# Row sums of a ReLU: two-pass steps of near-equal length, a partly fused sixth transfer, and another split of the last row between two engines

## The chip, the cores and the metric

The kernel runs on one core of a Trainium2 chip. The metric is the device time of one execution in microseconds (us). An execution also has a traced span, which is shorter than its time; the difference is called "time less span" below.

## The reference

```python
x = np.random.randn(32, 512, 1024).astype(np.float32)
def reference(x):
    return np.sum(np.maximum(x, 0), axis=-1).astype(np.float32)
```

67.1 MB are read and 64 KB are written. Each of 128 partitions holds 128 rows of 1024 numbers.

## The kernel before

The 128 rows of a partition arrive in seven transfers of 16 rows (three buffers in turn), then in pieces of 8, 4, 2 and 1 rows, then the last row as two halves. SyncE issues all transfers on one queue.

There are two ways to do a row. In two passes, ScalarE writes the ReLU back for several rows in one instruction and VectorE adds them up with one reduce. Fused, one instruction of either engine does ReLU and sum of one row, and leaves the sum in an accumulator that a short second instruction reads out.

```python
STEPS = [2, 6, 8]
TAIL = [8, 4, 2, 1]
LAST = [512, 512]
# ... allocation, and the transfers on SyncE: transfer c waits for s_dve of transfer c - 3 ...

    for c in range(NTWO):                      # transfers 1 to 6: two passes
        b, r = c % NB, 0
        act.wait_ge(s_in[c], 16)
        for i, n in enumerate(STEPS):
            t = buf[:, b, r : r + n, :]
            act.activation(t, t, AF.Relu).then_inc(s_act, 1)
            dve.wait_ge(s_act, len(STEPS) * c + i + 1)
            dve.tensor_reduce(out=res[...], in_=t, axis=X, op=ALU.add).then_inc(s_dve, 1)
            r += n
    # ... on_act(t, acc), on_dve(t, acc): the fused row on ScalarE, on VectorE ...
    for c in range(NTWO, NBIG):                # transfer 7: fused, rows in turn
        act.wait_ge(s_in[c], 16)
        dve.wait_ge(s_in[c], 16)
        for i in range(BIG):
            f = on_act if i % 2 else on_dve
            f(buf[:, c % NB, i, :], res[...])
    for r, n, s in tail:                       # pieces of 8, 4, 2, 1 rows: the same,
        act.wait_ge(s, 16)                     # the single row on ScalarE
        if n > 1:
            dve.wait_ge(s, 16)
        for i in range(r, r + n):
            f = on_act if n == 1 or (i - r) % 2 else on_dve
            ...
    last_act.then_inc(s_tact, 1)

    dve.wait_ge(s_in[-2], 16)                  # last row, first half: VectorE
    on_dve(buf[:, tb, BIG - 1, 0 : LAST[0]], last[:, LAST[1] : LAST[1] + 1]).then_inc(s_part, 1)
    dve.wait_ge(s_part, 1)
    dve.wait_ge(s_in[-1], 16)                  # second half and the partial sum beside it
    on_dve(last[:, :], res[:, J - 1 : J]).then_inc(s_tdve, 1)

    sp.wait_ge(s_tact, 1)
    sp.wait_ge(s_tdve, 1)
    sp.dma_start(out=ov[:, :], in_=res[:, :]).then_inc(s_out, 16)
```

Of the kernel before, what the change touches and what calls it, by code (L numbers as in the profile page):

```python
# [2 lines left out]

P = 128
D = 1024
BIG = 16
NBIG = 7
NTWO = 6
NB = 3
STEPS = [2, 6, 8]  # L10
TAIL = [8, 4, 2, 1]
LAST = [512, 512]


def bass_relu_sum_kernel(
    nc: bass.Bass,
    x: bass.AP,
    out: bass.AP,
):




    fp32 = mybir.dt.float32
    ALU = mybir.AluOpType
    AF = mybir.ActivationFunctionType
    X = mybir.AxisListType.X

    B, S, _ = x.shape
    J = B * S // P  # L30
    assert BIG * NBIG + sum(TAIL) + 1 == J and sum(LAST) == D

    xv = x.rearrange("b s d -> (b s) d").rearrange("(p j) d -> p j d", p=P)
    ov = out.rearrange("b s -> (b s)").rearrange("(p j) -> p j", p=P)

    buf = nc.alloc_sbuf_tensor("buf", [P, NB, BIG, D], fp32)
    last = nc.alloc_sbuf_tensor("last", [P, LAST[1] + 1], fp32)
    res = nc.alloc_sbuf_tensor("res", [P, J], fp32)

    n_in = NBIG + len(TAIL) + 2  # L40
    s_in = [nc.alloc_semaphore(f"s_in{i}") for i in range(n_in)]
    s_act = nc.alloc_semaphore("s_act")
    s_dve = nc.alloc_semaphore("s_dve")
    s_part = nc.alloc_semaphore("s_part")
    s_tact = nc.alloc_semaphore("s_tact")
    s_tdve = nc.alloc_semaphore("s_tdve")
    s_out = nc.alloc_semaphore("s_out")

    sp, act, dve = nc.sync, nc.scalar, nc.vector


    tb = NBIG % NB
    for c in range(NBIG + 1):
        if c >= NB:
            sp.wait_ge(s_dve, len(STEPS) * (c - NB + 1))
        if c < NBIG:
            sp.dma_start(  # L57
                out=buf[:, c % NB, :, :], in_=xv[:, c * BIG : (c + 1) * BIG, :]
            ).then_inc(s_in[c], 16)
    r = 0  # L60
    tail = []
    for i, n in enumerate(TAIL):
        sp.dma_start(
            out=buf[:, tb, r : r + n, :],
            in_=xv[:, NBIG * BIG + r : NBIG * BIG + r + n, :],
        ).then_inc(s_in[NBIG + i], 16)
        tail.append((r, n, s_in[NBIG + i]))
        r += n
    sp.dma_start(
        out=buf[:, tb, r, 0 : LAST[0]], in_=xv[:, J - 1, 0 : LAST[0]]  # L70
    ).then_inc(s_in[-2], 16)
    sp.dma_start(out=last[:, 0 : LAST[1]], in_=xv[:, J - 1, LAST[0] : D]).then_inc(
        s_in[-1], 16
    )


    for c in range(NTWO):
        b, r = c % NB, 0
        act.wait_ge(s_in[c], 16)
        for i, n in enumerate(STEPS):  # L80
            t = buf[:, b, r : r + n, :]
            act.activation(t, t, AF.Relu).then_inc(s_act, 1)  # L82
            dve.wait_ge(s_act, len(STEPS) * c + i + 1)
            dve.tensor_reduce(  # L84
                out=res[:, c * BIG + r : c * BIG + r + n], in_=t, axis=X, op=ALU.add
            ).then_inc(s_dve, 1)
            r += n


    def on_act(t, acc):  # L90
        return act.activation(t, t, AF.Relu, accum_out=acc)  # L91

    def on_dve(t, acc):
        return dve.tensor_scalar(  # L94
            out=t, in0=t, scalar1=0.0, scalar2=None, op0=ALU.max, op1=ALU.add, accum_out=acc
        )

    j0 = NBIG * BIG
    for c in range(NTWO, NBIG):
        act.wait_ge(s_in[c], 16)  # L100
        dve.wait_ge(s_in[c], 16)
        for i in range(BIG):
            f = on_act if i % 2 else on_dve
            f(buf[:, c % NB, i, :], res[:, c * BIG + i : c * BIG + i + 1])
    for r, n, s in tail:
        act.wait_ge(s, 16)
        if n > 1:
            dve.wait_ge(s, 16)
        for i in range(r, r + n):
            f = on_act if n == 1 or (i - r) % 2 else on_dve  # L110
            ins = f(buf[:, tb, i, :], res[:, j0 + i : j0 + i + 1])
            if f is on_act:
                last_act = ins
    last_act.then_inc(s_tact, 1)

    dve.wait_ge(s_in[-2], 16)
    on_dve(buf[:, tb, BIG - 1, 0 : LAST[0]], last[:, LAST[1] : LAST[1] + 1]).then_inc(s_part, 1)
    dve.wait_ge(s_part, 1)
    dve.wait_ge(s_in[-1], 16)
    on_dve(last[:, :], res[:, J - 1 : J]).then_inc(s_tdve, 1)  # L120


    sp.wait_ge(s_tact, 1)
    sp.wait_ge(s_tdve, 1)
    sp.dma_start(out=ov[:, :], in_=res[:, :]).then_inc(s_out, 16)
    sp.wait_ge(s_out, 16)


# [1 line left out]
_INS = ['x']  # L130
_OUTS = [((32, 512), 'float32')]


# [21 lines left out]
```

## Time and profile before

| | before |
|---|---|
| time, median of 3 | 164.67 us (164.54 to 165.19) |
| traced span of the profiled execution | 162.82 us |
| input queue's share of 16 DMA engines | 96.1% |
| seventh transfer taken up by ScalarE | 139.32 us |
| VectorE done with the sixth transfer | 142.72 us |
| final VectorE instruction starts | 160.46 us |

The page of the kernel before, its engines and its queue (busy us, share of the span, records; then packets, MB, share):

```profile
DVE 123.1 (76%) x52; ACT 102.7 (63%) x51; POOL 0.2 (0%) x4
...
q1 hardware_dynamic: 2016, 67.18, 96.1%
```

The queue is full and no engine is. Large transfers land 19.36 us apart, which is 433 GB/s (8.39 MB each). The Trainium skill, "DMA: Bandwidth & Descriptors", Specifications, gives a fabric ceiling of 435 GB/s, and this trace stays just below it. As long as the stream stays as it is, only what comes after the last landing can be shortened.

The timeline of the kernel before, cut to what the end needs (start us, duration us, engine, line, operation, operands, count, idle time before and what ended it):

```profile
119.96 14.04 ACT L82 ACTIVATE buf<-buf 128x2048 f32<-128x2048 f32 x3 [5.31 <-DMA buf<-in_x_dram]
...
134.03 8.69 DVE L84 TENSOR_REDUCE res<-buf 128x8 f32<-128x8192 f32 x1 [0.36 <-ACT buf L82]
139.32 1.06 ACT L91 ACTIVATE buf<-buf 128x1024 f32<-128x1024 f32 x1 [5.32 <-DMA buf<-in_x_dram]
...
142.64 1.21 DVE L94 TENSOR_SCALAR_CACHE_REDUCE buf<-buf 128x1024 f32<-128x1024 f32 x1
...
158.59 1.21 DVE L94 TENSOR_SCALAR_CACHE_REDUCE buf<-buf 128x1024 f32<-128x1024 f32 x1
...
159.73 0.68 DVE L94 TENSOR_SCALAR_CACHE_REDUCE buf<-buf 128x512 f32<-128x512 f32 x1
...
160.46 0.69 DVE L94 TENSOR_SCALAR_CACHE_REDUCE last<-last 128x513 f32<-128x513 f32 x1
161.07 0.08 DVE L94 DVE_READ_ACCUMULATOR last<-last 128x1 f32 x1
161.24 0.35 SPq L125 DMA_DIRECT2D out_dram<-res  x1
```

The seventh transfer has landed by 139.32, where ScalarE takes it up, but VectorE reduces the sixth until 142.72. From there on it does a row every 1.14 us and its instructions carry no idle time in brackets: it has a backlog. The last half row lands at about 158.9 (issued at 125.71, 33.2 us to landing), and VectorE comes to it 1.5 us later. Its line among the DMA issues (size, us from issue to landing):

```profile
last<-in_x_dram SPq DMA_DIRECT2D x1, 256.0 KB, 33.2
```

The waits of VectorE in the kernel before (us in total, times, longest) say the same: it never waited for a transfer.

```profile
DVE res L84 <- ACT buf L82: 38.0, 13, 25.1
```

So does the chain of work that ended last (start, us, what). After the sixth transfer's last reduce it is VectorE's own work:

```profile
134.03 8.69 DVE res L84
142.72 16.28 DVE buf L94 x29
...
160.46 0.69 DVE last L94 x2
```

### The profile page before, as it was taken

What the parts mean: (1) busy time and instruction counts of PE and PEld (TensorE: products, weight loads), DVE (VectorE), ACT (ScalarE), POOL (GpSimd) and SP (SyncE); (2) the same over time, 40 slices, a digit from 0 to 9 for tenths busy, and PEclk for the clock granted to TensorE, in tenths of its full rate; (3) what the DMA queues carried; (4) which work ended last, traced back from release to release, by engine and by line L of the source; (5) the groups of instructions that cost most, each with busy time, mean ns of one, the idle gap of its engine ahead of it and who ended that gap; (6) DMA issues with size and microseconds to landing.
All of it is one profiled execution on the core that took longest, in us unless ns stands there. A gap on an engine that the chain in (4) does not pass through costs nothing.

```text
span 162.8 us, 136 instructions
## 1 busy us (share of the span) xinstructions
DVE 123.1 (76%) x52; ACT 102.7 (63%) x51; POOL 0.2 (0%) x4
## 2 busy tenths in 40 slices
DVE  0000005599988999599996999969998799999995
ACT  3000039991599807996099942999159990796880
POOL 0000000000000000000000000000000000000000
DMA  7979979979989998998997997997998997999980
GB/s 258 515 306 467 499 322 467 515 322 451 515 370 403 515 419 354 515 419 354 515 467 306 515 499 322 467 515 338 435 515 354 419 515 338 427 419 403 411 322 16
DMA packets 2016, 67.18 MB, mean 413 GB/s; under 512 B 224, under 2 KB 352, under 8 KB 736
## 3 DMA queue, kind: packets, MB, share of 16 engines
q1 hardware_dynamic: 2016, 67.18, 96.1%
HBM read 67.11 MB, written 0.07 MB: 413 GB/s over the span
## 4 chain that ended last, share of the span: by engine, by line
DMA 47%; ACT 26%; DVE 22%; another core or an unknown queue 3%; issue 1%; SPq 0%
DMA buf<-in_x_dram 47%; ACT buf L82 26%; DVE res L84 11%; DVE buf L94 10%; DVE last L94 0%; SPq L57 0%
## 5 line engine op out<-in xcount | busy, mean ns | idle before, releaser
L84 DVE TENSOR_REDUCE res<-buf 128x2 f32<-128x2048 f32 (+2 forms) x18 | 104.7, 5839 | 38.0 <-ACT buf L82 38.0
L82 ACT ACTIVATE buf<-buf 128x2048 f32<-128x2048 f32 (+2 forms) x18 | 84.2, 4743 | 47.7 <-DMA buf<-in_x_dram 47.7
L91 ACT ACTIVATE buf<-buf 128x1024 f32<-128x1024 f32 x16 | 16.7, 1045 | 7.7 <-DMA buf<-in_x_dram 7.5
L94 DVE TENSOR_SCALAR_CACHE_REDUCE buf<-buf 128x1024 f32<-128x1024 f32 (+1 forms) x16 | 17.8, 1180 | 0.0
L91 ACT ACTIVATION_READ_ACCUMULATOR buf<-buf 128x1 f32 x16 | 3.0, 187 | 0.0
L82 ACT ACT_TABLE_LOAD x1 | 1.3, 1283 | 0.7 <-PEq L140 0.7
L94 DVE DVE_READ_ACCUMULATOR buf<-buf 128x1 f32 x16 | 1.3, 82 | 0.0
L94 DVE TENSOR_SCALAR_CACHE_REDUCE last<-last 128x513 f32<-128x513 f32 x1 | 0.7, 690 | 0.0
L140 POOL MEMSET const-bfloat16-1.0<- 128x1 bf16 x1 | 0.1, 102 | 0.0
L140 POOL MEMSET const-uint8-127<- 128x1 uint8 x1 | 0.1, 101 | 0.0
L140 POOL MEMSET const-float32-0.0<- 128x1 f32 x1 | 0.1, 99 | 0.2 <-issue 0.2
L140 POOL MEMSET const-float32-1.0<- 128x1 f32 x1 | 0.1, 98 | 0.0
L94 DVE DVE_READ_ACCUMULATOR last<-last 128x1 f32 x1 | 0.1, 82 | 0.0
## 6 DMA issues: line engine op xcount, KB each, us to landing
buf<-in_x_dram SPq DMA_DIRECT2D x1, 4096.0 KB, 25.6
buf<-in_x_dram SPq DMA_DIRECT2D x1, 2048.0 KB, 30.1
buf<-in_x_dram SPq DMA_DIRECT2D x1, 1024.0 KB, 32.1
buf<-in_x_dram SPq DMA_DIRECT2D x1, 512.0 KB, 32.9
buf<-in_x_dram SPq DMA_DIRECT2D x1, 256.0 KB, 33.1
last<-in_x_dram SPq DMA_DIRECT2D x1, 256.0 KB, 33.2
buf<-in_x_dram SPq DMA_DIRECT2D x7, 35.3
out_dram<-res SPq DMA_DIRECT2D x1, 64.0 KB, 1.5
```

The lines of the kernel that those rows point to most:

```text
L82: act.activation(t, t, AF.Relu).then_inc(s_act, 1)
L84: dve.tensor_reduce(out=res[:, c * BIG + r : c * BIG + r + n], in_=t, axis=X, op=ALU.add).then_inc(s_dve, 1)
L91: return act.activation(t, t, AF.Relu, accum_out=acc)
L94: return dve.tensor_scalar(out=t, in0=t, scalar1=0.0, scalar2=None, op0=ALU.max, op1=ALU.add, accum_out=acc)
L140: nc = _bacc.Bacc("TRN2", target_bir_lowering=False, num_devices=1)
```

## The change

The steps of the two-pass transfers become 4, 5, 7, so that the last reduce is shorter. In the sixth transfer only 12 rows go in two passes (3, 4, 5), and VectorE and ScalarE do two fused rows each. The single-row piece goes to VectorE. ScalarE does the last row's first half and hands its partial sum to VectorE's final instruction. The output transfer now waits for one semaphore, since the final instruction implies the rest.

```diff
-STEPS = [2, 6, 8]
+STEPS = [4, 5, 7]
+MIXED = [3, 4, 5]
 ...
+    for c in range(NTWO):
+        b, steps = c % NB, STEPS if c < NTWO - 1 else MIXED
+        act.wait_ge(s_in[c], 16)
+        if steps is MIXED:
+            dve.wait_ge(s_in[c], 16)
+            for i in (BIG - 4, BIG - 3):
+                on_dve(*row(c, i))
+        # ... the steps, as before ...
+        if steps is MIXED:
+            for i in (BIG - 2, BIG - 1):
+                on_act(*row(c, i))
 ...
-            f = on_act if n == 1 or (i - r) % 2 else on_dve
+            f = on_act if (i - r) % 2 else on_dve
 ...
-    dve.wait_ge(s_in[-2], 16)
-    on_dve(buf[:, tb, BIG - 1, 0 : LAST[0]], last[:, LAST[1] : LAST[1] + 1]).then_inc(s_part, 1)
-    dve.wait_ge(s_part, 1)
+    act.wait_ge(s_in[-2], 16)
+    on_act(buf[:, tb, BIG - 1, 0 : LAST[0]], last[:, LAST[1] : LAST[1] + 1]).then_inc(s_tact, 1)
+    dve.wait_ge(s_tact, 1)
     dve.wait_ge(s_in[-1], 16)
     on_dve(last[:, :], res[:, J - 1 : J]).then_inc(s_tdve, 1)
 
-    sp.wait_ge(s_tact, 1)
     sp.wait_ge(s_tdve, 1)
```

More of the change, by code (lines that the diff above doesn't have):

```diff
@@ L43, in bass_relu_sum_kernel @@
     s_dve = nc.alloc_semaphore("s_dve")
-    s_part = nc.alloc_semaphore("s_part")
     s_tact = nc.alloc_semaphore("s_tact")
@@ L54, in bass_relu_sum_kernel @@
         if c >= NB:
-            sp.wait_ge(s_dve, len(STEPS) * (c - NB + 1))
+            sp.wait_ge(s_dve, 3 * (c - NB + 1))
         if c < NBIG:
@@ L74, in bass_relu_sum_kernel @@
     )
-    for c in range(NTWO):
-        b, r = c % NB, 0
-        act.wait_ge(s_in[c], 16)
-        for i, n in enumerate(STEPS):
-            t = buf[:, b, r : r + n, :]
-            act.activation(t, t, AF.Relu).then_inc(s_act, 1)
-            dve.wait_ge(s_act, len(STEPS) * c + i + 1)
-            dve.tensor_reduce(
-                out=res[:, c * BIG + r : c * BIG + r + n], in_=t, axis=X, op=ALU.add
-            ).then_inc(s_dve, 1)
-            r += n
     def on_act(t, acc):
@@ L96, in on_dve, with row @@
         )
+    def row(c, i):
+        return buf[:, c % NB, i, :], res[:, c * BIG + i : c * BIG + i + 1]
+    for c in range(NTWO):
[5 more added lines that the diff above has]
+                on_dve(*row(c, i))
+        r = 0
+        for i, n in enumerate(steps):
+            t = buf[:, b, r : r + n, :]
+            act.activation(t, t, AF.Relu).then_inc(s_act, 1)
+            dve.wait_ge(s_act, 3 * c + i + 1)
+            dve.tensor_reduce(
+                out=res[:, c * BIG + r : c * BIG + r + n], in_=t, axis=X, op=ALU.add
+            ).then_inc(s_dve, 1)
+            r += n
+        if steps is MIXED:
+            for i in (BIG - 2, BIG - 1):
+                on_act(*row(c, i))
     j0 = NBIG * BIG
@@ L102, in bass_relu_sum_kernel @@
         for i in range(BIG):
-            f = on_act if i % 2 else on_dve
-            f(buf[:, c % NB, i, :], res[:, c * BIG + i : c * BIG + i + 1])
+            (on_act if i % 2 else on_dve)(*row(c, i))
     for r, n, s in tail:
-        act.wait_ge(s, 16)
         if n > 1:
-            dve.wait_ge(s, 16)
+            act.wait_ge(s, 16)
+        dve.wait_ge(s, 16)
         for i in range(r, r + n):
-            f = on_act if n == 1 or (i - r) % 2 else on_dve
-            ins = f(buf[:, tb, i, :], res[:, j0 + i : j0 + i + 1])
-            if f is on_act:
-                last_act = ins
-    last_act.then_inc(s_tact, 1)
-    dve.wait_ge(s_in[-2], 16)
-    on_dve(buf[:, tb, BIG - 1, 0 : LAST[0]], last[:, LAST[1] : LAST[1] + 1]).then_inc(s_part, 1)
-    dve.wait_ge(s_part, 1)
+            f = on_act if (i - r) % 2 else on_dve
+            f(buf[:, tb, i, :], res[:, j0 + i : j0 + i + 1])
+    act.wait_ge(s_in[-2], 16)
+    on_act(buf[:, tb, BIG - 1, 0 : LAST[0]], last[:, LAST[1] : LAST[1] + 1]).then_inc(s_tact, 1)
+    dve.wait_ge(s_tact, 1)
     dve.wait_ge(s_in[-1], 16)
     on_dve(last[:, :], res[:, J - 1 : J]).then_inc(s_tdve, 1)
-    sp.wait_ge(s_tact, 1)
     sp.wait_ge(s_tdve, 1)
```

## The prediction

> **What bounds it.** The input stream. The page's queue part gives one queue 67.18 MB, 96.1% of 16 engines' span. The timeline shows ScalarE released by each 8.39 MB transfer at 23.15, 42.45, 61.91, 81.28, 100.61, 119.96 and 139.32 us: 19.36 us apart, 433 GB/s. The Trainium skill, "DMA: Bandwidth & Descriptors", Specifications, gives a fabric ceiling of 435 GB/s; the trace agrees, so no compute order can speed up the stream. The queue never runs dry: the fourth transfer is issued at 45.93 us, when the first buffer is free, while the third is in flight until 61.91. What can be won is only what follows the last landing.
>
> **The end.** From issue and time to landing (DMA issues), the last row's first half lands near 158.33 us and its second near 158.92. The final VectorE instruction starts only at 160.46, so about 1.5 us is lost. The reason is backlog: the sixth transfer's last reduce (8 rows, 8.69 us) runs until 142.72, 3.4 us after the seventh landed. From 142.64 VectorE runs rows 1.14 us apart without a gap to 160.4 (groups: idle before 0.0). ScalarE is idle before each tail piece and done at 158.8.
>
> **What the change does.**
> 1. Steps 4,5,7. Reduce durations (by form: 2278, 6553, 8686 ns for 2, 6, 8 rows) fit about 145 + 1.043 ns per element: 4.42, 5.49, 7.62 us. ScalarE's fit the skill's "ScalarE: Activation LUTs" figure of 186 ns + 0.833 per element (8192: 7010 against 7012 ns measured), so its total stays about 14.05 us. VectorE's last reduce starts where it did (landing + 14.06), but is 7.6 instead of 8.7 us: VectorE ends about 21.7 us after a landing, not 22.75. The buffers come free 1 us earlier; nobody waits for them, so this is worth about 0 by itself.
> 2. Sixth transfer: VectorE, free 2.35 us after landing (119.96), does two fused rows (2.3 us), then reduces of 3, 4, 5 rows (3.35 + 4.42 + 5.49): done near 137.9 instead of 142.72, thus before the seventh lands. ScalarE finishes 12 + 2 rows at about 132.5. This removes the backlog.
> 3. Seventh: eight rows on VectorE 139.35 to 148.5, idle till 149.03; then four rows to about 153.65, two from 153.95 to 156.2, one from 156.43 to 157.65; the single-row piece (now VectorE) 157.67 to 158.9. It keeps pace with the landings.
> 4. The first half goes to ScalarE: starts near 158.36; estimate 0.61 us plus accumulator read, ending near 159.08. VectorE's final instruction waits for this (about 0.15 us longer than for its own landing), runs 159.1 to 159.8, against 160.46 to 161.15.
>
> On the critical path: about 1.35 us in total, nearly all from item 2 together with 3 and 4; the remainder of the changes is hidden under the stream. Without 4, the half row (0.6 us) and final would end near 160.2, so 4 is worth about 0.4 of it.
>
> **Prediction.** Span 162.8 to 161.45; the time 164.67 to 163.3 us (0.8% faster). Range 162.9 to 163.9. Faster by over 2%: 0.02; within 2%: 0.97; slower by over 2%: 0.01.
>
> **What would show it.** Landings of all seven large transfers unchanged within 0.1 us or so; VectorE's last reduce done near 138; VectorE idle before the seventh transfer and before each tail piece; final instruction starting near 159.1, released by ScalarE; chain of waits ending DMA, ScalarE half row, VectorE final.
>
> **What would make it wrong.** A stream whose landings shift (by the earlier issues, or by chance) by more than 0.5 us; VectorE not done with the single-row piece by 159.1; the accumulator reaching VectorE later than ScalarE's fit says; or a spread between runs (164.54 to 165.19 before) that hides a gain of this size.

## The result, and the profile after

| | before | after |
|---|---|---|
| time, median | 164.61 us (4 runs) | 162.93 us (4 runs, 162.74 to 163.03) |
| ratio, 95% interval | | 0.9889 (0.9864 to 0.9913) |
| traced span, profiled execution | 162.82 us | 161.37 us |
| time less span, profiled execution | 1.74 us | 1.55 us |

A ratio here is the mean time of one kernel's runs over that of the other's in the same rounds, so it is not quite the ratio of the medians. The prediction's own ratio, 163.3 over 164.67, is 0.9917: just outside this interval. The gain is larger than foretold. The median of 162.93 us lies at the lower edge of the stated range of 162.9 to 163.9; 0.9889 of the 164.67 us from which the prediction started would be 162.84, just below it.

The timeline of the changed kernel, for the same stretch:

```profile
119.92 10.63 ACT L99 ACTIVATE buf<-buf 128x3072 f32<-128x3072 f32 x3 [5.30 <-DMA buf<-in_x_dram]
122.19 1.21 DVE L82 TENSOR_SCALAR_CACHE_REDUCE buf<-buf 128x1024 f32<-128x1024 f32 x1
...
124.47 13.07 DVE L101 TENSOR_REDUCE res<-buf 128x3 f32<-128x3072 f32 x3
...
139.27 1.22 DVE L82 TENSOR_SCALAR_CACHE_REDUCE buf<-buf 128x1024 f32<-128x1024 f32 x1 [1.74 <-DMA buf<-in_x_dram]
...
157.65 1.22 DVE L82 TENSOR_SCALAR_CACHE_REDUCE buf<-buf 128x1024 f32<-128x1024 f32 x1
158.31 0.63 ACT L79 ACTIVATE buf<-buf 128x512 f32<-128x512 f32 x1 [0.80 <-DMA buf<-in_x_dram]
...
158.85 0.19 ACT L79 ACTIVATION_READ_ACCUMULATOR buf<-buf 128x1 f32 x1
159.07 0.69 DVE L82 TENSOR_SCALAR_CACHE_REDUCE last<-last 128x513 f32<-128x513 f32 x1 [0.19 <-ACT buf L79]
159.68 0.08 DVE L82 DVE_READ_ACCUMULATOR last<-last 128x1 f32 x1
159.79 0.35 SPq L132 DMA_DIRECT2D out_dram<-res  x1
```

VectorE is done with the sixth transfer at 137.54 (124.47 + 13.07) and waits 1.74 us for the seventh: the backlog is gone. At the end ScalarE's half row releases the final instruction at 159.07. The prediction had 137.9 and 159.1.

VectorE's waits in the changed kernel now name the transfers:

```profile
DVE res L101 <- ACT buf L99: 34.9, 10, 26.8
DVE buf L82 <- DMA buf<-in_x_dram: 2.5, 3, 1.7
DVE last L82 <- ACT buf L79: 0.2, 1, 0.2
```

The end of the chain that ended last, in the changed kernel (start, us, what), runs as foretold: landing, ScalarE, final instruction.

```profile
124.16 34.13 DMA buf<-in_x_dram
158.29 0.02 issue
158.31 0.73 ACT buf L79 x2
159.04 0.02 issue
159.07 0.69 DVE last L82 x2
```

The page of the changed kernel:

```profile
DVE 122.0 (76%) x56; ACT 101.0 (63%) x55; POOL 0.2 (0%) x4
...
q1 hardware_dynamic: 2016, 67.18, 97.0%
```

So the trace is almost exactly what was predicted, and the time is not. Note x52 and x56 in the two pages: VectorE has four records (instructions in the trace) more: two fused rows, two records each. That seemed to be of no interest.

### The profile page after: what moved, and what is told of

Its sections match the earlier page's. It is cut to its first block, busy times and chain, and to the rows that moved or that the text cites. A ratio compares the mean times of both kernels' runs of the same rounds, so it can differ in the third digit from the quotient of the medians.

```text
span 161.4 us, 143 instructions
## 1 busy us (share of the span) xinstructions
DVE 122.0 (76%) x56; ACT 101.0 (63%) x55; POOL 0.2 (0%) x4
## 4 chain that ended last, share of the span: by engine, by line
DMA 69%; ACT 18%; DVE 10%; SPq 1%; issue 0%
DMA buf<-in_x_dram 69%; ACT buf L99 17%; DVE res L101 9%; SPq L64 1%; ACT buf L79 0%; DVE last L82 0%; SPq L58 0%
## 5 line engine op out<-in xcount | busy, mean ns | idle before, releaser
L101 DVE TENSOR_REDUCE res<-buf 128x4 f32<-128x4096 f32 (+3 forms) x18 | 100.4, 5603 | 34.9 <-ACT buf L99 34.9
L99 ACT ACTIVATE buf<-buf 128x4096 f32<-128x4096 f32 (+3 forms) x18 | 80.8, 4553 | 47.7 <-DMA buf<-in_x_dram 47.7
L79 ACT ACTIVATE buf<-buf 128x1024 f32<-128x1024 f32 (+1 forms) x18 | 18.4, 1021 | 9.7 <-DMA buf<-in_x_dram 9.7
L82 DVE TENSOR_SCALAR_CACHE_REDUCE buf<-buf 128x1024 f32<-128x1024 f32 x18 | 21.0, 1217 | 2.7 <-DMA buf<-in_x_dram 2.5
```

Of the source, the lines that this page charges most:

```text
L79: return act.activation(t, t, AF.Relu, accum_out=acc)
L82: return dve.tensor_scalar(out=t, in0=t, scalar1=0.0, scalar2=None, op0=ALU.max, op1=ALU.add, accum_out=acc)
L101: dve.tensor_reduce(out=res[:, c * BIG + r : c * BIG + r + n], in_=t, axis=X, op=ALU.add).then_inc(s_dve, 1)
```

## The experiments

Eighteen experiments ran. Three of them (again, again_2, again_3) are the changed kernel itself, and one kernel ran twice (three_pieces). The seventh transfer is taken up between 139.08 and 139.55 us from profile to profile, so spans of two profiles differ by some tenths through the stream alone. To take that out, the column "end" is the start of the final VectorE instruction less the start of the first ScalarE instruction on the seventh transfer. "Out" is the time from the end of the final instruction's accumulator read to the output transfer's issue. Both are from the profiled execution. "Time less span" is the mean over the kernel's own timed executions. "Records" are VectorE's.

| kernel | end, us | out, us | records | time less span, us | ratio (95%) |
|---|---|---|---|---|---|
| before | 21.14 | 0.09 | 52 | 1.73 | 1 |
| after | 19.80 | 0.03 | 56 | 1.53 | 0.9889 (0.9864 to 0.9913) |
| again | 19.80 | 0.03 | 56 | 1.61 | 0.9910 (0.9896 to 0.9924) |
| again_2 | 19.79 | 0.03 | 56 | 1.57 | 0.9905 (0.9890 to 0.9920) |
| again_3 | 19.78 | 0.04 | 56 | 1.56 | 0.9899 (0.9885 to 0.9914) |
| steps_only | 20.05 | 0.10 | 52 | 1.74 | 0.9934 (0.9921 to 0.9948) |
| fused_only | 19.79 | 0.09 | 56 | 1.61 | 0.9907 (0.9893 to 0.9920) |
| half_only | 20.42 | 0.03 | 50 | 1.70 | 0.9953 (0.9940 to 0.9967) |
| end_only | 21.57 | 0.02 | 52 | 1.75 | 1.0020 (1.0005 to 1.0034) |
| fused_end | 19.79 | 0.03 | 56 | 1.61 | 0.9908 (0.9893 to 0.9922) |
| half_reduce | 19.78 | 0.10 | 52 | 1.75 | 0.9909 (0.9895 to 0.9924) |
| after_two_waits | 19.80 | 0.10 | 56 | 1.53 | 0.9902 (0.9886 to 0.9917) |
| before_one_wait | 21.14 | 0.03 | 52 | 1.74 | 0.9996 (0.9983 to 1.0010) |
| before_padded | 21.14 | 0.09 | 58 | 1.34 | 0.9972 (0.9955 to 0.9988) |
| before_padded_act | 21.15 | 0.09 | 53 | 1.73 | 1.0013 (0.9998 to 1.0028) |
| after_padded_2 | 19.79 | 0.03 | 58 | 1.36 | 0.9894 (0.9878 to 0.9911) |
| after_padded_4 | 19.79 | 0.03 | 60 | 1.33 | 0.9906 (0.9892 to 0.9921) |
| after_padded | 20.17 | 0.03 | 62 | 1.35 | 0.9911 (0.9896 to 0.9926) |
| three_pieces | 20.00 | 0.02 | 58 | 1.34 | 0.9890 (0.9875 to 0.9904) |
| three_pieces_2 | 19.99 | 0.03 | 58 | 1.38 | 0.9883 (0.9868 to 0.9898) |

The kernel before has 1.73 as the mean of 43 executions that ran beside the experiments, all between 1.68 and 1.77.

"Time less span" is a mean, and it hides a spread (spans to 0.1 us). Single executions lie between 1.65 and 1.79 us with 50 to 53 records, between 1.30 and 1.40 with 58 or more, but between 1.32 and 1.72 in the seven runs with 56.

### again: the changed kernel itself

No edit.

> The changed kernel once more, unaltered, against the kernel before, for a firm size. In the two traces the final VectorE instruction starts 1.39 us earlier and the span is 1.45 us shorter, but the medians differ by 1.68 us. Theory 1 (the trace holds nearly all of it; the rest was the spread of four runs): 1.4 to 1.5 us shorter, ratio about 0.991. Theory 2 (some 0.2 us is saved outside the traced span too): again 1.6 to 1.7 us shorter, ratio 0.990, and time less span is about 1.55 us for this kernel against 1.74 for the kernel before.

Measured: 163.04 us against 164.46 (medians), ratio 0.9910. The time was 1.47 us shorter by the means. Theory 1 looked right at first. But theory 2's second sign is there too: time less span is 1.61 us here (four executions, 1.53 to 1.68), 1.73 in the nine executions of the kernel before (1.68 to 1.76).

### steps_only

```diff
-STEPS = [2, 6, 8]
+STEPS = [4, 5, 7]
```

> The kernel before with steps 4,5,7 in place of 2,6,8 and nothing else. The prediction on record says worth about 0 by itself, because nobody waits for the buffers. Rival (backlog theory): the last two-pass reduce of the sixth transfer is 7.62 instead of 8.69 us and ends at 141.65, and VectorE, which has no gap after that, hands the 1.07 us straight to the end: 15 rows from 141.57 to 158.67, half row, final instruction starting at 159.40, span 1.06 us shorter. If the backlog theory is right the two effects of the change do not add up, since fusing alone removes the same backlog.

Measured: 163.46 us against 164.46, ratio 0.9934, span 161.73. The end is 1.09 us earlier. The timeline of this kernel:

```profile
134.01 7.62 DVE L84 TENSOR_REDUCE res<-buf 128x7 f32<-128x7168 f32 x1 [0.58 <-ACT buf L82]
...
141.54 1.21 DVE L94 TENSOR_SCALAR_CACHE_REDUCE buf<-buf 128x1024 f32<-128x1024 f32 x1
...
159.36 0.69 DVE L94 TENSOR_SCALAR_CACHE_REDUCE last<-last 128x513 f32<-128x513 f32 x1
```

The last reduce is 1.07 us shorter, every row after it starts 1.1 us earlier, and so does the final instruction. The prediction's "about 0 by itself" was wrong. It had looked at who waits for the buffers, and had overlooked that VectorE's own queue of work was waiting.

### fused_only

```diff
+MIXED = [3, 4, 5]
+# the changed kernel's loop over the first six transfers; STEPS stay 2, 6, 8 and the end stays as before
```

> The kernel before with the sixth transfer partly fused (steps 3,4,5, two fused rows on each engine) and nothing else; steps 2,6,8 for the first five, the last row's halves both on VectorE. Prediction on record: the hand-over of the half to ScalarE is worth about 0.4 us of 1.35, so this should bring about 0.95. Backlog theory, worked out again with landings: VectorE finishes the sixth transfer near 139.0, before the seventh lands at 139.3, keeps pace, starts the half row at 158.36 and the final instruction at 159.09, so 1.37 us, the same as the whole change, and the hand-over is worth 0 to 0.1.

Measured: 162.99 us against 164.46, ratio 0.9907, final instruction at 159.09. This part alone brings what the whole change brings. In its timeline VectorE waits for the half row and does it itself, without loss:

```profile
139.30 1.22 DVE L82 TENSOR_SCALAR_CACHE_REDUCE buf<-buf 128x1024 f32<-128x1024 f32 x1 [0.67 <-DMA buf<-in_x_dram]
...
158.36 0.69 DVE L82 TENSOR_SCALAR_CACHE_REDUCE buf<-buf 128x512 f32<-128x512 f32 x1 [0.73 <-DMA buf<-in_x_dram]
...
159.09 0.69 DVE L82 TENSOR_SCALAR_CACHE_REDUCE last<-last 128x513 f32<-128x513 f32 x1
```

From the half row's start to the final instruction's it is 0.73 us on VectorE here and 0.76 us on ScalarE in the changed kernel. The 0.4 us that the prediction gave to the hand-over was not there.

### half_only

```diff
 # shortened
-    last_act.then_inc(s_tact, 1)
 ...
-    dve.wait_ge(s_in[-2], 16)
-    on_dve(first half).then_inc(s_part, 1)
-    dve.wait_ge(s_part, 1)
+    act.wait_ge(s_in[-2], 16)
+    on_act(first half).then_inc(s_tact, 1)
+    dve.wait_ge(s_tact, 1)
 ...
-    sp.wait_ge(s_tact, 1)
```

> The kernel before with only the last row's first half moved from VectorE to ScalarE (the single-row piece stays on ScalarE, as before). VectorE keeps its backlog of 15 rows to 159.8 and is spared the half row's 0.61 to 0.7 us: final instruction at 159.8, span about 0.65 us shorter, plus up to 0.06 us because the output DMA then waits for one semaphore only. If instead the final instruction is bound by ScalarE or by its landing, it starts at 159.1 and the gain is 1.4.

Measured: 163.66 us against 164.46, ratio 0.9953, end 0.72 us earlier. The final instruction started at 159.67, not at 159.80, because it could follow the preceding row at the usual 1.14 us. With a backlog, moving the half row is worth its length.

### end_only

```diff
 # half_only, and the single-row piece too:
-            f = on_act if n == 1 or (i - r) % 2 else on_dve
+            f = on_act if (i - r) % 2 else on_dve
```

> The kernel before with the whole new end (half row on ScalarE and the single-row piece on VectorE), but its old steps and an unfused sixth transfer. Backlog theory: VectorE still carries its backlog from 142.64 and now has 16 whole rows at 1.14 us instead of 15 and a half row, so the final instruction starts near 160.85 instead of 160.46: slower by 0.3 to 0.4 us in the span (less 0.06 to 0.09 for the output DMA that waits for one semaphore). If the end were worth 0.4 us as the prediction says, it would be faster by that.

Measured: 164.91 us against 164.63, ratio 1.0020, end 0.43 us later. The new end by itself, on a VectorE with a backlog, is a small loss: 1.14 us of row came, 0.7 us of half row went.

### fused_end

```diff
 # the changed kernel with
-STEPS = [4, 5, 7]
+STEPS = [2, 6, 8]
```

> The changed kernel with steps 2,6,8 in the first five transfers: that is, the change without its near-equal steps. Backlog theory: steps matter only while VectorE's backlog reaches the end; with the sixth transfer fused it ends at 139.0 instead of 137.9, still before the seventh lands (139.3), so the final instruction stays near 159.07 and the span near 161.37; ratio equal to that of the changed kernel within 0.001. If the steps act on the stream or add up, it is slower by about 1 us.

Measured: 163.02 us against 164.44, ratio 0.9908, end 19.79, as in the changed kernel. Once the sixth transfer is partly fused, the steps are worth nothing. So the parts do not add up: they all remove the same backlog, and the first one that removes it takes the whole gain.

### half_reduce (wrong result)

```diff
-                in_=t, axis=X, op=ALU.add
+                in_=t[:, :, 0:512] if (c, i) == (5, 2) else t, axis=X, op=ALU.add
```

> Wrong on purpose (8 columns of the result are sums of half a row): the kernel before, whose last two-pass reduce of the sixth transfer reads only the first 512 elements of each row, 4.4 instead of 8.7 us. This removes VectorE's backlog with every instruction count kept. Backlog theory: VectorE is done with the sixth transfer near 138.5, idle until the seventh lands, final instruction at 159.09, span 1.35 us shorter, as with the fused sixth transfer. Time less span: gap theory about 1.6 us, length theory 1.73.

Measured: wrong result as intended, 163.05 us against 164.53, ratio 0.9909, end 19.78. All else is the kernel before. Taking 4.3 us from one reduce in the sixth transfer moves the end as far as the whole change does, and no farther. The timeline of this kernel:

```profile
133.81 4.42 DVE L84 TENSOR_REDUCE res<-buf 128x8 f32<-128x4096 f32 x1 [0.37 <-ACT buf L82]
...
139.09 1.22 DVE L94 TENSOR_SCALAR_CACHE_REDUCE buf<-buf 128x1024 f32<-128x1024 f32 x1 [0.86 <-DMA buf<-in_x_dram]
...
158.86 0.69 DVE L94 TENSOR_SCALAR_CACHE_REDUCE last<-last 128x513 f32<-128x513 f32 x1
```

VectorE now waits 0.86 us for the seventh transfer. That settles the backlog as the cause of the earlier end (21.14 to 19.78). Time less span stayed at 1.75 us, so the missing backlog does not change that.

### after_two_waits and before_one_wait

```diff
 # after_two_waits: the changed kernel and
+    sp.wait_ge(s_tact, 1)
     sp.wait_ge(s_tdve, 1)
```

```diff
 # before_one_wait: the kernel before, with
     dve.wait_ge(s_part, 1)
+    dve.wait_ge(s_tact, 1)
 ...
-    sp.wait_ge(s_tact, 1)
```

> The changed kernel with one needless wait of the output DMA on ScalarE's semaphore put back. In the traces the output DMA follows the final instruction by 0.09 us with two waits and by 0.03 us with one. If the number of waits does that: 0.06 us later, span 161.43 to 161.45, final instruction unmoved. If the last 0.2 us of the first comparison hung on this too, 0.2 us or more slower in time than the changed kernel.

> The kernel before, with ScalarE's semaphore awaited by VectorE ahead of its final instruction (long satisfied by then) instead of by the output DMA. If the number of waits matters: output DMA 0.02 to 0.03 us after the final instruction, span 162.76 instead of 162.82, possibly given back by a later start of the final instruction. If something else set the 0.09 us: unchanged.

Measured: "out" is 0.09 or 0.10 us in all seven kernels with two semaphores on the output transfer and 0.02 to 0.04 us in all the others. So the second wait costs about 0.06 us, though its semaphore had long been set. In time that is too little to show: before_one_wait has a ratio of 0.9996, after_two_waits has 0.9902. It does not account for the remaining 0.16 us.

### three_pieces and three_pieces_2

```diff
-LAST = [512, 512]
+LAST = [512, 256, 256]      # ScalarE, VectorE, and VectorE's final with both partial sums
```

> A try at beating the changed kernel: the last row in three pieces of 512 (ScalarE), 256 (VectorE) and 256 elements plus the two partial sums (VectorE, final). The final instruction then takes 258 instead of 513 elements: worked out from 690 ns at 513 and 1214 ns at 1024, about 430 ns instead of 690. It can start about 0.2 us after the last landing, when the middle piece's partial is there, against 0.15 us now: end 0.2 us earlier, span near 161.2. If the smaller transfers land later by more than 0.2 us, no gain.

> The three-piece end once more, beside the changed kernel on the same chip. In its trace the final instruction ended about 0.08 us sooner after the landings than in the changed kernel, not 0.2, because VectorE was still on the single-row piece when the middle piece landed. So 0 to 0.2 us faster than the changed kernel in the same rounds; more would not be explained by the trace.

Measured: 162.83 us, ratio 0.9890, and 162.53 us, ratio 0.9883 (again_2, in the same rounds as the second: 162.89 us, 0.9905). The final instruction took 0.42 instead of 0.69 us but started 0.2 us later. It ended 0.08 us sooner, counted from the seventh transfer. That was about all that the first trace could explain, and the time was shorter by more. Both runs had the lowest time less span so far, 1.34 and 1.38 us, and VectorE had 58 records. This made the number of records a suspect.

### before_padded and before_padded_act

```diff
+    pad = nc.alloc_sbuf_tensor("pad", [P, 6], fp32)
+    for i in range(6):
+        dve.memset(pad[:, i : i + 1], 0.0)       # before_padded; before_padded_act: six tiny ACTIVATEs
```

> The kernel before with six 1-column memsets on VectorE at its very start, in the 25 us for which VectorE waits anyway. Time less traced span is 1.73 us in the kernel before and in all variants with 50 to 52 VectorE records, 1.53 to 1.61 in those with 56, 1.34 to 1.38 in those with 58. Length theory (the number of instructions in VectorE's program sets what is spent outside the span): 1.35 to 1.6 us here, so the time is 0.15 to 0.4 us shorter with the same span. Gap theory (what counts is that VectorE has no backlog at the end): 1.73 us and the same time.

> The same padding on ScalarE: six 1-column ACTIVATEs at its start, and one memset on VectorE that feeds them. If ScalarE's program counts as VectorE's does: time less span below 1.6 us. If only VectorE's counts, or the gaps do: 1.70 to 1.75 us.

Measured: before_padded ran in 164.12 us against 164.53, ratio 0.9972 (0.9955 to 0.9988). Six instructions more made the kernel 0.4 us faster, with the end at 21.14 as ever; time less span fell from 1.73 to 1.34 us. All four executions (163.98 to 164.24) lie below all seven of the kernel before on the same chip (164.41 to 164.67). The memsets took 0.20 us at 0.80, where VectorE waits for data anyway. Padding ScalarE did nothing of the kind: 1.73 us, ratio 1.0013. So the count of VectorE's instructions matters.

### after_padded, after_padded_2, after_padded_4

The same edit on the changed kernel, with six, two and four memsets.

> The changed kernel with the same six memsets on VectorE at the start (62 records there). Span unchanged at 161.2 to 161.4. Length theory, if it is steady: time less span below 1.4 us. Gap theory: 1.5 to 1.6 us, as without them.

> The changed kernel, unaltered, as the standard for the two padded ones on the same chip: span 161.2 to 161.5 us, time less span 1.5 to 1.65 us, ratio 0.9905.

> The changed kernel with two 1-column memsets on VectorE at its start: 58 records, as in the three kernels so far with 1.34 to 1.38 us outside the span and no stall within it. Theory: some step of VectorE's instruction stream that costs about 0.4 us sits at a fixed distance in the stream; with 50 to 52 records it falls wholly behind the last work (1.73 us outside), with 56 partly, with 58 not at all. Then: time less span 1.35 us, span as the changed kernel's, so 0.2 us faster than it. If the three-piece kernel's gain came from its shorter final instruction alone: no gain here.

> Four memsets, 60 records. With six (62) the final instruction started 0.40 us after ScalarE's partial was there instead of 0.03, and time less span was 1.35: the 0.4 us had moved into the span. With four the step lies two records later in the program than with six: either still ahead of the final instruction (span 0.4 us longer, no gain over the unpadded one), or between it and the end (span unchanged, 1.35 outside, as with two).

Measured: with two memsets time less span is 1.36 us and the end is unmoved, as the length theory has it. The time is 162.71 us against 162.86 for the unpadded kernel on the same chip (again_3); the intervals of the ratios overlap, so this difference is not settled as a gain in time. With four, time less span is 1.33 us, but in the profiled execution the output transfer took 1.7 us from issue to landing instead of 1.5 (so it did in before_padded), and nothing is left (162.93 us). With six, the cost shows up inside the span. The timeline of after_padded:

```profile
158.23 0.63 ACT L82 ACTIVATE buf<-buf 128x512 f32<-128x512 f32 x1 [0.81 <-DMA buf<-in_x_dram]
...
158.76 0.19 ACT L82 ACTIVATION_READ_ACCUMULATOR buf<-buf 128x1 f32 x1
159.35 0.69 DVE L85 TENSOR_SCALAR_CACHE_REDUCE last<-last 128x513 f32<-128x513 f32 x1 [0.56 <-ACT buf L82]
```

ScalarE's read ended at 158.95, yet the final instruction started 0.40 us later; in the changed kernel that gap is 0.03 us. The timeline puts the wait down to ScalarE, which had been done for 0.40 us. The chain that ended last names nothing for it ("issue" is time in which the engine waited for nothing that the profile shows):

```profile
158.23 0.73 ACT buf L82 x2
158.96 0.39 issue
159.35 0.69 DVE last L85 x2
```

The trace's list of DMA packets hints at what. Besides data it holds packets of 8 KB of the kind "instruction". The last of them start at these times from the span's start (the span ends between 161.1 and 163.1):

```text
                         VectorE records   last 8 KB instruction packet listed, us
before, steps_only, half_only,
  end_only, half_reduce,
  before_one_wait         50 to 52          none near the end
the seven with 56         56                162.60 to 162.95, 1.4 us past their spans' ends
after_padded_2            58                161.32
three_pieces (two)        58                160.83 and 161.27
after_padded_4            60                160.18
after_padded              62                160.25
before_padded             58                162.36, before its span's end at 162.90
```

The Trainium skill, "Runtime: NRT & Kernel Launch", Instruction fetch mechanics, says that each engine's instructions are fetched in 16 KiB blocks while earlier ones execute, and that crossing a block costs one small queue operation, "mostly hidden". The runs fit this in part: against the end of its own span, the packet comes 1.4 us after it with 56 records, 0 to 0.5 us before it with 58 and 1.4 us before it with 60 and 62, so it comes sooner the more instructions VectorE has. But the packet is half a block, and in after_padded it starts 0.9 us after the delayed final instruction had started, so the packet itself did not hold that instruction up; whether the request for it did, the trace does not tell. Nor do the packets say which engine fetched them (before_padded_act, with ScalarE padded, has one at 164.36), and no run takes the fetch away. That the count of VectorE's instructions moves a cost of about 0.4 us is shown. That the fetch is this cost is not.

## Why the prediction was right or wrong

**What bounds it: right.** The stream did not move. Large transfers land at most 0.05 us apart between the two first traces, and no experiment brought the seventh before 139.08.

**The mechanism: right.** The backlog of VectorE set the end. It is gone in the changed kernel, and half_reduce, which removes nothing but the backlog, moves the end by the same amount.

**The predicted end: right.** Final instruction at 159.1 predicted, 159.07 measured; span 161.45 predicted, 161.37 measured. With the drift of the stream taken out, the end moved by 1.34 us (21.14 to 19.80); "about 1.35 us in total" was predicted.

**The failed step: "Span 162.8 to 161.45; the time 164.67 to 163.3 us".** The prediction took the shortening of the chain to be the shortening of the time, that is, it took time less span to stay where it was. That term was mis-sized: time less span fell from 1.73 to 1.57 us. Over all 16 timed executions of the changed kernel and the 43 of the kernel before beside the experiments, the means are 162.94 and 164.54 us: 1.60 us, not 1.37. It is made up as follows.

| part | us | from |
|---|---|---|
| final instruction earlier | 1.34 | "end", 21.14 to 19.80 |
| output transfer follows it sooner | 0.06 | "out", 0.09 to 0.03: one semaphore fewer |
| time less span | 0.16 | 1.73 to 1.57, mean of 16 executions |
| not traced (in the first two profiles the seventh transfer was taken up 0.05 us sooner) | 0.04 | rest |

The third part is the larger miss. It came with two fused rows more on VectorE, four records: all seven runs with 56 have it (1.53 to 1.61), while half_reduce, with the same end and 52 records, has not (1.75). That instructions alone can do this is shown by before_padded, where six tiny ones took 0.39 us off the time outside the span. The chain of waits cannot show it, as it lies outside the span.

The first comparison showed more still, 1.83 us by its means. The three later ones gave 0.9910, 0.9905 and 0.9899, so about 0.2 us of that is put down to the spread of four runs each (one run before was at 165.19). Two of the three later intervals hold the predicted 0.9917, the third (0.9885 to 0.9914) does not.

**"Worth about 0 by itself" for the steps: wrong.** They alone shorten the end by 1.09 us. **"4 is worth about 0.4": wrong.** Without it the end is at 19.79, the same. Both slips were hidden in the sum, because the parts overlap: whichever removes the backlog first gets the gain.

**Still open.** What precisely costs the 0.4 us. Why single executions scatter so widely with 56 records. Whether a kernel with 58 VectorE records is truly faster in time than the changed one. All four executions of three_pieces_2 (162.45 to 162.60) lie below all four of again_2 in the same rounds (162.69 to 163.22), but it also has another end and, in these executions, a shorter span. after_padded_2, which differs by the records alone, had 162.71 against 162.86, and there the single executions overlap.

## What to carry to other kernels

When one engine runs without a gap to the end, look back to where its backlog began: what is taken out anywhere since then arrives at the end, until the engine meets a landing (here 1.07 us out of a reduce moved the end by 1.09, and 4.3 us moved it by no more than 1.36), and parts of a change that remove the same backlog must not be added up. A prediction in device time should compare time less span between variants too; where it differs by a constant amount, the cause lies outside the traced work, and padding an idle engine with a few tiny instructions is a cheap test. For an effect of 1%, two sets of four runs were not enough here to judge the forecast: they gave 1.83 us, where all runs together give 1.60.

## What the Trainium skill lacked or had wrong

- "Runtime: NRT & Kernel Launch", Instruction fetch mechanics, calls the crossing of a block "mostly hidden". Here up to 0.4 us depended on the number of VectorE's instructions: time less span was 1.70 to 1.75 us with 50 to 53 records, 1.53 to 1.61 with 56 (means; single executions 1.32 to 1.72), 1.33 to 1.38 with 58 or more; with 62, 0.4 us appeared ahead of the final instruction. If the fetch is the cause, the page lacks that it can be exposed at a kernel's end.
- No page tells that a second semaphore on a transfer costs time even when it has long been set: 0.09 to 0.10 us from the final instruction to the output transfer's issue with two, 0.02 to 0.04 us with one.
- "VectorE: DVE Perf Modes", The perf-mode tier table, lists `tensor_scalar` on fp32 at 2x, 1227 ns for 2048 elements. The form that also sums up took 1214 ns for 1024 elements, half that rate, and 690 ns for 513; this table does not mention the form, though other pages of the skill keep it apart from the plain one.
- "ScalarE: Activation LUTs", What ACT_TABLE_LOAD costs, was right to within 0.02 us: its 186 ns plus 0.833 ns per element (for immediate scale and bias) give an estimate of 612 ns for 512 elements, and 612 and 630 ns were measured (half_only and the changed kernel). It lacks the time of the accumulator read that follows, 187 ns here.
